# Two-instruction products of mLSTM weights and values over a pair of PSUM banks, and 512-column output banks in the projections of a hybrid encoder layer

## The chip, the cores and the metric

The kernel runs on one core of a Trainium2 chip. The metric is device time in microseconds (us) of one execution. Before the change the median of three runs is 2720.48 us (2719.08 to 2722.17).

## The reference, cut to what matters

One encoder layer is applied to two sequences, `x_prompt` (1024 tokens) and `x_sample` (2048 tokens), each with 16 learned meta tokens in front. A combined input projection (1024 to 6672 columns) feeds two branches, a neighbourhood attention and a bidirectional mLSTM; each is gated, projected, merged with the other by sigmoid gates and sent through one output projection with a normalisation and a residual.

```python
xn = _rmsnorm(h, g_pre)
proj = xn @ w_in + b_in.astype(xn.dtype)
...
ya = (ya.reshape(B, L, NA_WIDTH) * jax.nn.silu(na_z)) @ w_a
yb = (_mlstm_branch(ml_qk, ml_v, ml_g, ml_o, ml_conv_w, ml_head_g) * jax.nn.silu(ml_z)) @ w_b
ga, gb = jnp.split(jax.nn.sigmoid(mg), 2, axis=-1)
y = (ga * ya + gb * yb) @ w_out
return h + _rmsnorm(y, g_post)
```

In the mLSTM, 4 heads of 128 run over the tokens in chunks, forward and backward. The output of a chunk has a part from within the chunk, the weighted scores `S` times the values, and a part from the state carried in from the other chunks:

```python
S = jnp.einsum('bhnjd,bhnsd->bhnjs', q, k) * jnp.exp(logD - m_t[..., None])
e_inter = jnp.exp(inter - m_t)
num = jnp.einsum('bhnjs,bhnsv->bhnjv', S, v) + e_inter[..., None] * jnp.einsum('bhnvk,bhnjk->bhnjv', Cs, q)
```

## The kernel before

**Numbers in two parts.** TensorE (PE) multiplies in a reduced float32 (`F32R`). To keep float32 accuracy, each operand is split into a high part (a copy by ScalarE, ACT) and a low part (the difference, by VectorE, DVE), and a product is three matmuls: high by high, high by low, low by high. `mm3` (L170 to L174) issues these three; the first operand is the one that is loaded into the array, the second is streamed.

**Dense and sparse work.** `run` interleaves two Python generators. `sparse` walks through `STEPS`: mLSTM of the short sequence, its attention, mLSTM of the long sequence, its attention. `dense` walks through `PLAN`: input projections of groups of 512 tokens, then `final` for each block of 512 tokens (two of the short sequence, four of the long one). Each `yield` names a cost, and `run` lets dense work follow sparse work in the ratio of `rate`. PE executes in exactly this program order (`manual_schedule`); the order on the other engines and on the DMA queue of SyncE (SP) is chosen by the scheduler from a simulation, and where `behind` is called it keeps program order.

**PSUM.** There are 8 banks of 512 columns of float32. `psum` (L166) hands them out by tag: `pj` has 3 (projections), `tr` has 2 (transposes and others), `sc` has 1 (scores), and `sm` has 2 (small products: gates, states, the products of `back`, and the attention's scores and outputs).

**mLSTM outputs.** `ml_outputs` goes over blocks of 256 tokens (`CB` = 2 chunks of 128). In five steps per block it runs `scores(b)`, `back(b-1, 0)` and `weigh(b)`, `split` and `mask`, `back(b-1, 1)` with `values(b)` and `state(b)`, then `decay` and `finish`; between the steps dense matmuls run. `scores` (L1799, L1801) multiplies keys and queries in a 256-column and a 128-column matmul for each chunk. `weigh` makes the weighted scores in parts `sh` and `sl`. `values` makes `vh` and `vl`, 130 columns for each chunk: 128 of values, one of ones for the denominator, one of zeros. `back` makes the state's part in a `tr` bank, scales it into `num` with ACT (L1829), then takes an `sm` bank and issues three 130-column matmuls for each of two directions; DVE adds all 260 columns to `num` at L1834. `finish` divides by the denominators. `ml_states` makes the states' increments in the same way, one `sm` bank for each chunk, read by ACT (L1715) and DVE (L1717).

**Token-major projections.** `tm_unit` (matmuls at L644 to L646) computes 256 or 264 columns of the projection for tiles of 128 tokens. Each tile takes a `pj` bank and is evacuated by one DVE addition of the bias (L661 for the long sequence); two tiles share one buffer `stT` and one store.

**The end of the layer.** `final` has two stages for each block of 512 tokens. The first projects both branches (`mm3` with 512 columns, weight units `("m", f)`) and merges them into `mh` and `ml`. The second, the out stage, multiplies by `w_out`: `prods` (L2042 to L2044) issues 12 matmuls of 256 columns for one token tile and one weight unit, `("o", c, a)`, where `c` is the quarter of the 1024 columns and `a` the half of the contraction. Before, the loop goes over quarters `cq`, halves `a`, and four token tiles; a quarter holds two banks, each with two token tiles. `leave` squares with ACT (L2047, summing for the norm) and multiplies by the gain with DVE (L2048). In the last block the last two quarters are done tile by tile.

**Weights.** `wpump` keeps at most four weight units (`NBW` = 4, buffers `whi` and `wlo`) in flight. The first use of a unit loads it raw, splits it, and stores both parts (512 KB each); later uses load both parts (L264, on SP). `wtake` hands out the next unit, `wdone` frees one and pumps.

Of the kernel before, what the change touches and what calls it, by code (L numbers as in the profile page):

```python
# [126 lines left out]
class K:  # L127
# [38 lines left out]
    def psum(self, tag, shape):  # L166
        return self.pp.tile(shape, F32, name=tag, tag=tag, bufs=BANKS[tag])

# [8 lines left out]
    def setup(self, ctx):  # L177
        tc, nc, i = self.tc, self.nc, self.i
        self.cp = cp = ctx.enter_context(tc.tile_pool(name="cp", bufs=1))
        self.dp = dp = ctx.enter_context(tc.tile_pool(name="dp", bufs=1, space=DRAM))  # L180
        self.pp = ctx.enter_context(tc.tile_pool(name="pp", bufs=2, space=PSUM))
        self.ident = cp.tile([P, P], F32, name="ident")
# [436 lines left out]
    def tm_unit(self, col, halves, wd):  # L619
# [10 lines left out]
        for j, (x, s, c, n, cnt, tok) in enumerate(todo):  # L630
            st = wp.tile([P, 2, WU], F32, name="stT", bufs=4)
            for a in range(cnt):
                p = self.psum("pj", [P, 512])
                o = p[:n, :wd]
                xs = slice(c + a * P, c + a * P + n)
                for k in range(KT):
                    wh, wl = ws[k // 4][0][:, k % 4, :], ws[k // 4][1][:, k % 4, :]
                    if tok is None:
                        both = [(p[:48, :wd], self.xmm[:, k, :], wh), (o, self.xmm[:, k, :NM], wl)]
                        for y, (out, lhs, rhs) in enumerate(both if k < KT - 1 else both[::-1]):  # L640
                            nc.tensor.matmul(out, lhs, rhs, start=k == y == 0, stop=k == KT - 1 and y == 1, skip_group_check=True)
                    else:
                        xh, xl = x[0][:, k, xs], x[1][:, k, xs]
                        nc.tensor.matmul(o, xh, wh, start=k == 0, stop=False)  # L644
                        nc.tensor.matmul(o, xh, wl, start=False, stop=False)  # L645
                        nc.tensor.matmul(o, xl, wh, start=False, stop=k == KT - 1)  # L646
# [10 lines left out]
                elif s == 0:  # L657
                    r = tok // P + a
                    nc.vector.scalar_tensor_tensor(st[:n, a, :wd], p[:n, :wd], self.rc[:n, r:r + 1], bb[:n, :wd], op0=ALU.mult, op1=ALU.add)
                else:  # L660
                    nc.vector.tensor_tensor(st[:n, a, :wd], p[:n, :wd], bb[:n, :wd], op=ALU.add)  # L661
                if a == cnt - 1:
                    self.tm_store(col, wd, s, n, cnt, tok, st)
# [764 lines left out]
    def ml_gates(self, s, keep, mp, res):  # L1428
# [34 lines left out]
        def one(d):  # L1463
            l2 = lf[:, d].rearrange("p c h -> p (c h)")
            pb = self.psum("sm", [P, 512])
            nc.tensor.matmul(pb[:, :NR], self.tri[:, d, :], l2, start=True, stop=True)
# [14 lines left out]
            end = P - 1 if d == 0 else 0  # L1481
            pg = self.psum("sm", [P, 512])
# [4 lines left out]
            px = self.psum("sm", [P, 512])  # L1487
            nc.tensor.transpose(px[0:1, :NR], cm[:, end:end + 1], self.ident[:NR, :NR])
# [14 lines left out]
            yield  # L1503
            pm = self.psum("sm", [P, 512])
            nc.tensor.transpose(pm[:NR, 0:1], mpv, self.ident[0:1, 0:1])
# [11 lines left out]
            yield  # L1517
            pu = self.psum("sm", [P, 512])
            nc.tensor.transpose(pu[:, :NR], uR, self.ident[:NR, :NR])
# [6 lines left out]
            for name, x in (("e", cm), ("w", aR)):  # L1526
                pe = self.psum("sm", [P, 512])
                nc.tensor.transpose(pe[:, :NR], x, self.ident[:NR, :NR])
# [3 lines left out]
                yield  # L1532
            pf = self.psum("sm", [P, 512])
            nc.tensor.matmul(pf[:, :NR], self.ones[:NR, :], dg, start=True, stop=True)
# [62 lines left out]
    def ml(self, s):  # L1597
# [3 lines left out]
        with tc.tile_pool(name=f"mg{s}", bufs=1, side="right", reuse_waits="tile") as keep:  # L1601
            with tc.tile_pool(name=f"mt{s}", bufs=1, side="right", reuse_waits="tile") as mp:
# [6 lines left out]
                yield from self.ml_gates(s, keep, mp, g)  # L1609
            with tc.tile_pool(name=f"ml{s}", bufs=1, side="right", reuse_waits="tile") as mp:  # L1610
                self.vas = [mp.tile([P, CB, 130], F32, name=f"va{j}") for j in range(3)]
# [19 lines left out]
                while norms:  # L1631
# [3 lines left out]
                    yield A_A  # L1635
        self.done.add(("ml", s))

    def vload(self, mp, s, h, tok, np_, nch):
# [7 lines left out]
    def ml_states(self, mp, s, h, g, NB, sts):  # L1646
# [34 lines left out]
        for i in range(N):  # L1681
# [25 lines left out]
            if b:  # L1707
                sts[b - 1] = mp.tile([P, CB, 260], F32, name="st", bufs=NB)
            for j in range(CB - 1, -1, -1):
                cc = b * CB + j  # L1710
                pd = self.psum("sm", [P, 512])
                self.mm3(pd[:, :260], kth[:, j, :], ktl[:, j, :],
# [8 lines left out]
    def ml_outputs(self, mp, s, h, g, NB, sts, norms):  # L1721
# [96 lines left out]
        def back(b, j):  # L1818
            sh, sl = shs[b]
            (vh, vl), qx = vs[b], qks[b][:, 0]  # L1820
            cch, ccl = cs[b]
# [6 lines left out]
            for d in range(2):  # L1828
                nc.scalar.activation(num[:, j, d], pi[:, 130 * d:130 * d + 130], AF.Copy, scale=g[d]["e"][:, cc, h:h + 1])  # L1829
            pa = self.psum("sm", [P, 512])  # L1830
# [3 lines left out]
            nc.vector.tensor_tensor(nj, pa[:, :260], nj, op=ALU.add)  # L1834

# [129 lines left out]
    def final(self, s, b, nxt):  # L1965
# [55 lines left out]
        yt = [fp.tile([P, D], F32, name="yo", tag="xr", bufs=4) for _ in range(4)]  # L2021
        ssq = fp.tile([P, 4, 4], F32, name="ssq", bufs=2)
        sqj = fp.tile([P, 256], mybir.dt.bfloat16, name="sqj", tag="thT", bufs=1)
        hook = None
# [20 lines left out]

        def leave(o, tt, cq):
            nc.scalar.activation(sqj, o, AF.Square, accum_out=ssq[:, tt, cq:cq + 1])  # L2047
            nc.vector.tensor_tensor(yt[tt][:, cq * 256:(cq + 1) * 256], o, self.gpost[:, cq * 256:(cq + 1) * 256], op=ALU.mult)  # L2048

        for cq in range(4 if nxt else 2):  # L2050
            banks = [self.psum("pj", [P, 2, 256]) for _ in range(2)]
            for a in range(2):
                w = self.wtake(1)[0]
                for tt in range(4):
                    prods(banks[tt // 2][:, tt % 2], tt, w, a, tt % 2 == 0)
                    if tt == 3:
                        self.wdone()
                    if a and tt % 2:
                        for t in (tt - 1, tt):
                            leave(banks[t // 2][:, t % 2], t, cq)  # L2060
                        if nxt and hook is None:
# [5 lines left out]
                    if hook:  # L2067
                        next(hook, None)
                    yield 12 * C256
        if not nxt:  # L2070
            ws = [[self.wtake(1)[0] for _ in range(2)] for _ in range(2)]
            for tt, cq in [(0, 2), (1, 2), (0, 3), (1, 3), (2, 2), (2, 3), (3, 2), (3, 3)]:
                o = self.psum("pj", [P, 512])[:, :256]
                for a in range(2):
                    prods(o, tt, ws[cq - 2][a], a, True)
                    if a == 0:
                        yield 12 * C256
                leave(o, tt, cq)
                if cq == 3:
# [187 lines left out]
```

## Time and profile before

| | |
|---|---|
| median of three runs | 2720.48 us |
| the profiled execution's own time | 2718.74 us |
| its span, first to last instruction | 2717.0 us |
| granted TensorE clock, mean | 0.998 |
| DMA | 657.53 MB, mean 242 GB/s |
| out stages of `final`, first start to last end of L2042 to L2044 | 2056.1 to 2117.5, 2177.1 to 2240.8, 2303.0 to 2370.4, 2431.7 to 2493.0, 2553.0 to 2614.9, 2662.8 to 2708.7 us |
| additions of L1834, starts of the first and the last | 665.8 and 1977.8 us |

Busy time counts the union of the instructions of an engine. Matmuls overlap, so a busy PE says that it wasn't waiting, and the price of a matmul is the distance to the start of the next one. "PEld" is the weight load, which runs beside matmuls. In a group line the columns are busy us, the mean ns of one, and the idle time of the engine before them with what ended it.

### The profile page before, as it was taken

Reading aid. Unit: us, or ns where it says so; the run is one execution under the profiler, and the core shown is the slowest. Engines: PE = TensorE matmul, PEld = TensorE weight load, DVE = VectorE, ACT = ScalarE, POOL = GpSimd, SP = SyncE. Lnnn points to the kernel's source line nnn. Section 1 sums busy time; section 2 is a strip of 40 time slices with the busy share of each in tenths; the row PEclk is TensorE's granted clock in tenths of the full one; section 3 lists DMA queues with packets and bytes.
Section 4 is the critical chain, followed back from the end, with each engine's and each line's share of the span. In section 5 each row is a group of like instructions: output and inputs, shape, how many; then the busy total and the mean of one; then the engine's idle time right before and its main releaser. Section 6 shows DMA issues by size and latency. Waiting matters only on the chain.

```text
span 2717.0 us, 47583 instructions
## 1 busy us (share of the span) xinstructions
PE 2686.7 (99%) x16696; PEld 2394.5 (88%) x16696; DVE 1766.1 (65%) x4376; ACT 1520.2 (56%) x3375; POOL 126.0 (5%) x294
## 2 busy tenths in 40 slices
PE   9999999999999999999999999999999999999998
PEld 7999988879998889998878888888879898989988
DVE  5557765535777747775424857574658879687864
ACT  5233354435555656666535757564648686767641
POOL 0005000005000013000000000000000000000000
PEclk9999999999999999999999999999999999999999
DMA  9984454369865797757486666786599999898955
GB/s 369 340 283 143 138 187 158 102 239 343 265 222 174 264 325 227 229 175 234 144 294 191 222 202 209 262 278 201 163 299 332 313 298 295 245 317 244 324 208 220
DMA packets 351507, 657.53 MB, mean 242 GB/s; under 512 B 53444, under 2 KB 158868, under 8 KB 351268
## 3 DMA queue, kind: packets, MB, share of 16 engines
q1 hardware_dynamic: 344004, 645.46, 71.7%
q0 software_dynamic: 7264, 9.04, 1.2%
q8 instruction: 131, 2.15, 0.3%
q14 instruction: 108, 0.88, 0.1%
HBM read 438.64 MB, written 215.66 MB: 241 GB/s over the span
## 4 chain that ended last, share of the span: by engine, by line
PE 88%; DMA 7%; DVE 2%; ACT 2%; issue 1%; SPq 1%; POOL 0%; DVEq 0%; ACTq 0%; POOLq 0%
PE pj L172 14%; PE pj L173 14%; PE pj L174 14%; PE pj L644 5%; PE pj L645 5%; PE pj L646 5%; PE sm L1407 3%; PE pj L2042 2%; PE pj L2044 2%; PE pj L2043 2%; PE tr L1393 2%; PE sm L174 2%; PE sm L173 2%; PE sm L172 2%; DMA wraw<-wu 1%; DMA wlo<-wl 1%
## 5 line engine op out<-in xcount | busy, mean ns | idle before, releaser
L172 PE MATMUL pj<-xh,whi 128*128 128x512 f32 (+1 forms) x1480 | 580.2, 392 | 4.6 <-ACT st L569 3.6
L173 PE MATMUL pj<-xl,whi 128*128 128x512 f32 (+1 forms) x1480 | 565.8, 382 | 0.2 <-DVE xl L345 0.2
L174 PE MATMUL pj<-xh,wlo 128*128 128x512 f32 (+1 forms) x1480 | 565.1, 382 | 0.3 <-DVE wlo L272 0.3
L644 PE MATMUL pj<-whi,xh 128*128 128x256 f32 (+1 forms) x1152 | 330.9, 287 | 0.0
L174 PEld LDWEIGHTS pj<-xh,wlo 128*128 128x128 f32 x1480 | 278.2, 188 | 58.2 <-DVE wlo L272 0.6
L172 PEld LDWEIGHTS pj<-xh,whi 128*128 128x128 f32 x1480 | 278.5, 188 | 54.1 <-ACT st L569 4.4
L645 PE MATMUL pj<-wlo,xh 128*128 128x256 f32 (+1 forms) x1152 | 325.0, 282 | 0.6 <-DMA wlo<-wl 0.6
L646 PE MATMUL pj<-whi,xl 128*128 128x256 f32 (+1 forms) x1152 | 324.8, 282 | 0.0
L173 PEld LDWEIGHTS pj<-xl,whi 128*128 128x128 f32 x1480 | 278.8, 188 | 46.2 <-issue 0.7
L2042 PE MATMUL pj<-whi,mh 128*128 128x256 f32 x768 | 220.3, 287 | 0.0
L645 PEld LDWEIGHTS pj<-wlo,xh 128*128 128x128 f32 x1152 | 217.1, 188 | 0.9 <-DMA wlo<-wl 0.8
L644 PEld LDWEIGHTS pj<-whi,xh 128*128 128x128 f32 x1152 | 217.3, 189 | 0.4
L646 PEld LDWEIGHTS pj<-whi,xl 128*128 128x128 f32 x1152 | 217.0, 188 | 0.0
L2043 PE MATMUL pj<-wlo,mh 128*128 128x256 f32 x768 | 217.0, 283 | 0.0
L2044 PE MATMUL pj<-whi,mlo 128*128 128x256 f32 x768 | 216.9, 282 | 0.0
L1396 DVE TENSOR_TENSOR pts<-tr,pts 96x384 fp32r<-96x384 f32 (+2 forms) x192 | 118.5, 617 | 64.7 <-ACT pts L1395 63.8
L172 PE MATMUL pj<-yh,whi 128*128 128x512 f32 x384 | 154.2, 401 | 1.8 <-DVE tg L2009 1.1
L173 PE MATMUL pj<-yl,whi 128*128 128x512 f32 x384 | 151.0, 393 | 0.2 <-DVE yl L1420 0.2
L174 PE MATMUL pj<-yh,wlo 128*128 128x512 f32 x384 | 151.0, 393 | 0.0
L2043 PEld LDWEIGHTS pj<-wlo,mh 128*128 128x128 f32 x768 | 146.1, 190 | 1.0
L2042 PEld LDWEIGHTS pj<-whi,mh 128*128 128x128 f32 x768 | 146.0, 190 | 1.0
L2044 PEld LDWEIGHTS pj<-whi,mlo 128*128 128x128 f32 x768 | 145.9, 190 | 0.0
(459 smaller groups left out, 6171.7 us busy)
## 6 DMA issues: line engine op xcount, KB each, us to landing
whi<-wh SPq DMA_DIRECT2D x140, 512.0 KB
wlo<-wl SPq DMA_DIRECT2D x140, 512.0 KB
wraw<-wu SPq DMA_DIRECT2D x64, 512.0 KB
wh<-whi SPq DMA_DIRECT2D x64, 512.0 KB
wl<-wlo SPq DMA_DIRECT2D x64, 512.0 KB
gt<-st SPq DMA_DIRECT2D x96, 256.0 KB
tg<-gt SPq DMA_DIRECT2D x96, 256.0 KB
xt<-xt SPq DMA_DIRECT2D x32, 512.0 KB
```

The source lines that it names most:

```text
L172: mm(out, ah, bh, start=start, stop=False, **more)
L173: mm(out, ah, bl, start=False, stop=False, **more)
L174: mm(out, al, bh, start=False, stop=stop, **more)
L644: nc.tensor.matmul(o, xh, wh, start=k == 0, stop=False)
L645: nc.tensor.matmul(o, xh, wl, start=False, stop=False)
L646: nc.tensor.matmul(o, xl, wh, start=False, stop=k == KT - 1)
L1393: nc.tensor.transpose(pt[:ks, ch, :], pr_[:, ch * ks:(ch + 1) * ks], self.ident)
L1396: nc.vector.tensor_tensor(pts[:ks, :nb, 1, :], pt[:ks, :nb], pts[:ks, :nb, 0, :].bitcast(F32), op=ALU.subtract)
L1407: nc.tensor.matmul(av[:, cb % 2], vt[:ks, kc // 8 + ch].rearrange("p a b -> p (a b)"), pts[:ks, ch].rearrange("p a b -> p (a b)"), start=c ...
L2042: nc.tensor.matmul(o, mh[:, f, xs], q, start=fresh and f == 0, stop=False, skip_group_check=True)
L2043: nc.tensor.matmul(o, mh[:, f, xs], w[1][:, k, :], start=False, stop=False, skip_group_check=True)
L2044: nc.tensor.matmul(o, ml[:, f, xs], q, start=False, stop=f == KT - 1, skip_group_check=True)
```

## The change

Four things change.

1. **The product of `back`.** High and low parts of the values stand side by side in one tile, 260 columns. For each direction, one matmul takes the low weights by the high values (130 columns), and one takes the high weights by 258 columns, high values and 128 columns of low values. Each direction has its own bank, in a two-bank tile `pa` with a single buffer, and DVE adds columns 0 to 130 and then columns 130 to 258 of both banks to `num`.
2. **The pool of small banks.** `sm` becomes a pool of its own. It is closed while the mLSTM runs, and the two banks are then one two-bank tile, which `ml_states` uses too (one bank for each chunk of a block). The small products of `ml_gates` go to `tr`.
3. **`tm_unit`.** Where two tiles fit into a bank (256 columns, long sequence), both go into one `pj` bank and one DVE addition evacuates both.
4. **The out stage of `final`.** The loop goes over halves of the columns (512), pairs of token tiles, and four weight units; each token tile has its own bank of 512 columns, and `leave` works on 512 columns. In the last block the second half is done tile by tile as before, with `ssq` of three columns.

```diff
     def psum(self, tag, shape):
-        return self.pp.tile(shape, F32, name=tag, tag=tag, bufs=BANKS[tag])
+        return (self.pm if tag == "sm" else self.pp).tile(shape, F32, name=tag, tag=tag, bufs=BANKS[tag])
+
+    def small(self, on):
+
+        if on:
+            self.sms = ExitStack()
+            self.pm = self.sms.enter_context(self.tc.tile_pool(name=f"pm{len(self.done)}", bufs=2, space=PSUM))
+        else:
+            self.sms.close()
...
+            pair = s and tok is not None and 2 * wd <= 512
             for a in range(cnt):
-                p = self.psum("pj", [P, 512])
-                o = p[:n, :wd]
+                if not pair or not a:
+                    p = self.psum("pj", [P, 512])
+                o = p[:n, wd * a:wd * a + wd] if pair else p[:n, :wd]
...
+                elif a:
+                    two = bb[:, :wd].rearrange("p (t c) -> p t c", t=1).to_broadcast([P, 2, wd])
+                    nc.vector.tensor_tensor(st[:, :, :wd], p[:, :2 * wd].rearrange("p (t c) -> p t c", t=2), two, op=ALU.add)
...
+            self.small(False)
+            with tc.tile_pool(name=f"ml{s}", bufs=1, side="right", reuse_waits="tile") as mp, \
+                 tc.tile_pool(name=f"pl{s}", bufs=1, space=PSUM) as self.pl:
...
+            pds = self.pl.tile([P, CB, 512], F32, name="pa")
             for j in range(CB - 1, -1, -1):
                 cc = b * CB + j
-                pd = self.psum("sm", [P, 512])
+                pd = pds[:, j]
...
-                vh = mp.tile([P, CB, 130], F32R, name="vh", bufs=1)
-                vl = mp.tile([P, CB, 130], F32R, name="vl", bufs=1)
-                nc.scalar.activation(f2(vh), f2(va), AF.Copy)
-                nc.vector.tensor_tensor(f2(vl), f2(va), f2(vh).bitcast(F32), op=ALU.subtract)
-                vs[b] = vh, vl
+                v = vs[b] = mp.tile([P, CB, 2, 130], F32R, name="vh", bufs=1)
+                nc.scalar.activation(v[:, :, 0], va, AF.Copy)
+                nc.vector.tensor_tensor(v[:, :, 1], va, v[:, :, 0].bitcast(F32), op=ALU.subtract)
...
-            pa = self.psum("sm", [P, 512])
+            pa = self.pl.tile([P, 2, 512], F32, name="pa")
             for d in range(2):
-                self.mm3(pa[:, 130 * d:130 * d + 130], sh[:, j, d, :], sl[:, j, d, :], vh[:, j, :], vl[:, j, :])
-            nj = num[:, j].rearrange("p d c -> p (d c)")
-            nc.vector.tensor_tensor(nj, pa[:, :260], nj, op=ALU.add)
+                nc.tensor.matmul(pa[:, d, 0:130], sl[:, j, d, :], v[:, j, 0], start=True, stop=False, skip_group_check=True)
+                nc.tensor.matmul(pa[:, d, 0:258], sh[:, j, d, :], v[:, j].rearrange("p a c -> p (a c)")[:, 0:258], start=False, stop=True, skip_group_check=True)
+            nj = num[:, j]
+            nc.vector.tensor_tensor(nj, pa[:, :, 0:130], nj, op=ALU.add)
+            nc.vector.tensor_tensor(nj[:, :, 0:P], pa[:, :, 130:258], nj[:, :, 0:P], op=ALU.add)
...
-        for cq in range(4 if nxt else 2):
-            banks = [self.psum("pj", [P, 2, 256]) for _ in range(2)]
-            for a in range(2):
-                w = self.wtake(1)[0]
-                for tt in range(4):
-                    prods(banks[tt // 2][:, tt % 2], tt, w, a, tt % 2 == 0)
-                    if tt == 3:
-                        self.wdone()
-                    if a and tt % 2:
-                        for t in (tt - 1, tt):
-                            leave(banks[t // 2][:, t % 2], t, cq)
...
+        for cp in range(2 if nxt else 1):
+            ws = []
+            for pair in range(2):
+                banks = [self.psum("pj", [P, 512]) for _ in range(2)]
+                for u in range(4):
+                    if not pair:
+                        ws.append(self.wtake(1)[0])
+                    for t in range(2):
+                        tt, o = 2 * pair + t, 256 * (u // 2)
+                        prods(banks[t][:, o:o + 256], tt, ws[u], u % 2, u == 0)
+                        if pair and t:
+                            self.wdone()
+                        if u == 3:
+                            leave(banks[t], tt, 512 * cp, 512, cp)
```

More of the change, by code (lines that the diff above doesn't have):

```diff
@@ L181, in setup @@
         self.pp = ctx.enter_context(tc.tile_pool(name="pp", bufs=2, space=PSUM))
+        for tag in ("pj", "tr", "sc"):
+            self.psum(tag, [P, 512])
+        self.small(True)
+        ctx.callback(lambda: self.small(False))
         self.ident = cp.tile([P, P], F32, name="ident")
@@ L643, in tm_unit @@
                         xh, xl = x[0][:, k, xs], x[1][:, k, xs]
-                        nc.tensor.matmul(o, xh, wh, start=k == 0, stop=False)
-                        nc.tensor.matmul(o, xh, wl, start=False, stop=False)
-                        nc.tensor.matmul(o, xl, wh, start=False, stop=k == KT - 1)
+                        nc.tensor.matmul(o, xh, wh, start=k == 0 and not (pair and a), stop=False, skip_group_check=True)
+                        nc.tensor.matmul(o, xh, wl, start=False, stop=False, skip_group_check=True)
+                        nc.tensor.matmul(o, xl, wh, start=False, stop=k == KT - 1, skip_group_check=True)
                     if k == 3:
@@ L659, in tm_unit @@
                     nc.vector.scalar_tensor_tensor(st[:n, a, :wd], p[:n, :wd], self.rc[:n, r:r + 1], bb[:n, :wd], op0=ALU.mult, op1=ALU.add)
-                else:
+                elif not pair:
                     nc.vector.tensor_tensor(st[:n, a, :wd], p[:n, :wd], bb[:n, :wd], op=ALU.add)
+                elif a:
+                    two = bb[:, :wd].rearrange("p (t c) -> p t c", t=1).to_broadcast([P, 2, wd])
+                    nc.vector.tensor_tensor(st[:, :, :wd], p[:, :2 * wd].rearrange("p (t c) -> p t c", t=2), two, op=ALU.add)
                 if a == cnt - 1:
@@ L1472, in one @@
             yield
-            pa = self.psum("sm", [P, 512])
+            pa = self.psum("tr", [P, 512])
             nc.tensor.transpose(pa[:NR, :P], aTf, self.ident)
@@ L1517, in one @@
             yield
-            pu = self.psum("sm", [P, 512])
+            pu = self.psum("tr", [P, 512])
             nc.tensor.transpose(pu[:, :NR], uR, self.ident[:NR, :NR])
@@ L1636, in ml @@
         self.done.add(("ml", s))
+        self.small(True)
     def vload(self, mp, s, h, tok, np_, nch):
@@ L1697, in ml_states @@
             if not c0:
-                pd = self.psum("sm", [P, 512])
+                pd = self.pl.tile([P, 2, 512], F32, name="pa")[:, 0]
                 self.mm3(pd[:, :130], kth[:NM, 0, :], ktl[:NM, 0, :], vwh[:NM, 0, 0, :], vwl[:NM, 0, 0, :])
@@ L1819, in back @@
             sh, sl = shs[b]
-            (vh, vl), qx = vs[b], qks[b][:, 0]
+            v, qx = vs[b], qks[b][:, 0]
             cch, ccl = cs[b]
@@ L2021, in final @@
         yt = [fp.tile([P, D], F32, name="yo", tag="xr", bufs=4) for _ in range(4)]
-        ssq = fp.tile([P, 4, 4], F32, name="ssq", bufs=2)
-        sqj = fp.tile([P, 256], mybir.dt.bfloat16, name="sqj", tag="thT", bufs=1)
+        ssq = fp.tile([P, 4, 3], F32, name="ssq", bufs=2)[:, :, :2 if nxt else 3]
+        sqj = fp.tile([P, 512], mybir.dt.bfloat16, name="sqj", tag="thT", bufs=1)
         hook = None
@@ L2044, in prods, with leave @@
                 nc.tensor.matmul(o, ml[:, f, xs], q, start=False, stop=f == KT - 1, skip_group_check=True)
[L2046 to L2061 removed]
+        def leave(o, tt, c0, n, q):
+            nc.scalar.activation(sqj[:, :n], o, AF.Square, accum_out=ssq[:, tt, q:q + 1])
+            nc.vector.tensor_tensor(yt[tt][:, c0:c0 + n], o, self.gpost[:, c0:c0 + n], op=ALU.mult)
+        for cp in range(2 if nxt else 1):
[12 more added lines that the diff above has]
+                            leave(banks[t], tt, 512 * cp, 512, cp)
+                        if nxt and hook is None and u == 2:
                             if nxt[0] != "f":
@@ L2066, in final @@
                                 hook = self.ystart(*nxt[1:])
-                    if hook:
-                        next(hook, None)
-                    yield 12 * C256
+                        if hook:
+                            next(hook, None)
+                        yield 12 * C256
         if not nxt:
@@ L2077, in final @@
                         yield 12 * C256
-                leave(o, tt, cq)
+                leave(o, tt, 256 * cq, 256, cq - 1)
                 if cq == 3:
```

15 lines of the change are left out of this document (6 added, 9 removed).

## The prediction

> **What bounds the kernel now.** I read the head of the profile first, then the groups by line with shapes kept apart, the order of time around one product, and the waits.
>
> ```profile
> span 2717.0 us, 47583 instructions
> PE 2686.7 (99%) x16696; PEld 2394.5 (88%) x16696; DVE 1766.1 (65%) x4376; ACT 1520.2 (56%) x3375; POOL 126.0 (5%) x294
> PE 88%; DMA 7%; DVE 2%; ACT 2%; issue 1%; SPq 1%; POOL 0%; DVEq 0%; ACTq 0%; POOLq 0%
> ```
>
> The tensor engine (PE) is idle for 2717.0 - 2686.7 = 30.3 us in all. So work taken off VectorE (DVE) or ScalarE (ACT) can give back at most a part of these 30 us, and matmul time taken off PE shortens the span directly, as long as nothing new makes PE wait. Three edits bear on time: the packed product in `back`, the shared banks of `tm_unit`, and the 512-column banks of `final`.
>
> **The packed product.** Before, `back` computes weights times values for each direction in three 130-column matmuls with three weight loads:
>
> ```profile
> L174 PE MATMUL sm<-vh,sl 128*128 128x130 f32 x192 | 52.9, 276 | 0.0
> L173 PE MATMUL sm<-vl,sh 128*128 128x130 f32 x192 | 52.7, 274 | 0.0
> L172 PE MATMUL sm<-vh,sh 128*128 128x130 f32 x192 | 48.0, 250 | 0.0
> ```
>
> 192 of each are 96 products of two directions (12 blocks of 256 tokens over both sequences, 4 heads, 2 chunks). The mean of one, 276 ns, is no price: matmuls overlap. The price is the distance between starts, which the order of time gives (start, duration):
>
> ```profile
> 663.96 0.23 PE L172 MATMUL sm<-vh,sh 128*128 128x130 f32 x1
> 664.03 0.27 PE L173 MATMUL sm<-vl,sh 128*128 128x130 f32 x1
> 664.14 0.28 PE L174 MATMUL sm<-vh,sl 128*128 128x130 f32 x1
> 664.25 0.28 PE L172 MATMUL sm<-vh,sh 128*128 128x130 f32 x1
> ...
> 664.58 0.33 PE L644 MATMUL pj<-whi,xh 128*128 128x256 f32 x1
> 664.75 0.28 PE L645 MATMUL pj<-wlo,xh 128*128 128x256 f32 x1
> 664.87 0.28 PE L646 MATMUL pj<-whi,xl 128*128 128x256 f32 x1
> ```
>
> Here 130 columns cost 0.11 us (664.03 to 664.14) and 256 columns 0.12 us (664.75 to 664.87). The narrow one is not paid by its columns but by the weight load that must come before the next matmul. The six take 664.58 - 663.96 = 0.62 us, and the dense matmul behind them starts its successor after 0.17 instead of 0.12 us, so the product costs 0.67 us. After the change each direction is one 130-column and one 258-column matmul. The trace has the same alternation, in the scores:
>
> ```profile
> 661.72 0.28 PE L1799 MATMUL sc<-qkx 128*128 128x256 f32 x1
> 661.84 0.22 PE L1801 MATMUL sc<-qkx 128*128 128x128 f32 x1
> 661.90 0.33 PE L1799 MATMUL sc<-qkx 128*128 128x256 f32 x1
> 662.07 0.22 PE L1801 MATMUL sc<-qkx 128*128 128x128 f32 x1
> 662.13 0.34 PE L644 MATMUL pj<-whi,xh 128*128 128x256 f32 x1
> 662.30 0.28 PE L645 MATMUL pj<-wlo,xh 128*128 128x256 f32 x1
> ```
>
> Four matmuls: 662.13 - 661.72 = 0.41, plus 0.05 behind them, is 0.46 us. I take 0.46 for the new product. The saving is 0.21 us, times 96 = 20 us. Its bounds: nothing, if the columns alone counted (390 before and 388 after), and 192 removed matmuls x 0.11 = 21 us, if the widening is free.
>
> [...]
>
> **What the packed product adds.** A second DVE addition folds columns 130 to 258 in, and both banks are now one tile with a single buffer, where two single-bank buffers took turns. So the product for chunk j=1 of a block must wait until both additions of chunk j=0 are done. Behind that matmul the whole PE queue waits, dense work included. The prices:
>
> ```profile
> L1834 DVE TENSOR_TENSOR num<-sm,num 128x260 f32<-128x260 f32 x96 | 40.5, 423 | 62.5 <-ACT num L1829 59.6 <-ACT vwh L1671 2.6
> 905.00:945.00 40.00, 40.00 (x213) 33.99 (x212) 37.66 (x103) 28.05 (x65) 2.92 (x12) 1.00 0.64 200
> 1763.08 0.22 PE L172 MATMUL sm<-vh,sh 128*128 128x130 f32 x1
> 1766.89 0.23 PE L172 MATMUL sm<-vh,sh 128*128 128x130 f32 x1
> 1764.17 0.43 DVE L1834 TENSOR_TENSOR num<-sm,num 128x260 f32<-128x260 f32 x1 [1.12 <-ACT num L1829]
> 915.08 0.23 PE L172 MATMUL sm<-vh,sh 128*128 128x130 f32 x1
> 918.90 0.22 PE L172 MATMUL sm<-vh,sh 128*128 128x130 f32 x1
> 921.95 0.75 DVE L1834 TENSOR_TENSOR num<-sm,num 128x260 f32<-128x260 f32 x2
> ```
>
> (The second line is a stretch: start and end, its length, then busy us of PE, weight loads, DVE, ACT and GpSimd, the granted clock, the DMA share and GB/s.) The usual pair of backs looks like the one at 1763: the addition ends at 1764.60, the next product starts at 1766.89, and a second addition of 0.42 still leaves 1.9 us. The exception is 905 to 945, the last head of the short sequence, where DVE is busy 37.66 of 40 us. The first product is at 915.08, the second at 918.90, and the addition comes only at 921.95, merged with the next one. With one buffer PE would stand until about 922.8, an estimate of 3.5 to 4 us. That stall lets DVE catch up, so it isn't paid at each of the four pairs there. The other check is DVE's work: 8 more additions x 0.42 = 3.4 us on 37.66 make 41.1 in a stretch that should shrink to 38. Both readings give 3 to 4 us; I add 1 to 2 for smaller ones elsewhere and take 5, between 0 (the scheduler, which orders DVE with the new wait in view, moves the additions forward) and 12 (each late pair pays in full).
>
> The states' products use the same pair of banks; their readers come at once, and the next block's products follow two steps of dense work later, so I cost them at nothing (cover: that dense work; without it each of the 48 blocks would wait for one more read of a bank, some 0.4 us by the row of L1834). The gates' small products move to tag "tr", which has two buffers as "sm" had: nothing.
>
> **The shared banks of `tm_unit`.** PE issues the same matmuls. For the long sequence's 256-wide columns two DVE additions become one:
>
> ```profile
> L661 DVE TENSOR_TENSOR stT<-pj,bb 128x256 f32<-128x256 f32 x96 | 40.3, 420 | 27.9 <-PE pj L646 26.2 <-DMA nv<-stT 0.6
> L1940 DVE TENSOR_TENSOR yl<-yl,yh 128x512 fp32r<-128x512 f32 x43 | 28.2, 682 | 1.5 <-ACT yh L1956 1.4
> L2048 DVE TENSOR_TENSOR yo<-pj,gain 128x256 f32<-128x256 f32 x96 | 40.3, 419 | 38.7 <-ACT sqj L2047 38.1
> ```
>
> 48 x (2 x 0.42 - 0.68) = 7.7 us of DVE work go, beside PE. A bank is asked for half as often. Nothing on the path.
>
> **The banks of `final`.** Again the same matmuls. The evacuations of 256 columns become 44 of 512 and 8 of 256, 7 us of DVE work less, nothing on the path by itself. What counts is when things come free. In the out stage each weight unit now serves two token tiles, then all four are used again by the other two. Before, a unit was read by four tiles in one go, and a freed buffer had the time of three more units to be refilled. Now four units are freed one after another in the second half, and each is needed three half-units later.
>
> ```profile
> 2056.00:2118.00 62.00, 61.02 (x508) 60.73 (x507) 49.81 (x114) 51.51 (x125) 0.00 (x0) 1.00 1.00 338
> 2553.00:2615.00 62.00, 61.66 (x508) 61.05 (x507) 41.32 (x103) 43.47 (x113) 0.00 (x0) 1.00 0.74 239
> 2663.00:2709.00 46.00, 45.72 (x384) 45.52 (x382) 17.23 (x64) 7.93 (x32) 0.00 (x0) 1.00 0.48 179
> kx<-masks POOLq DMA_DIRECT2D x2, 256.0 KB, 6.2
> ACT sqj L2047 <- PE pj L2044: 43.9, 28, 7.1
> DVE yo L2048 <- ACT sqj L2047: 38.1, 39, 7.2
> ```
>
> The out stage takes 62 us for 8 units, 7.75 us each, so the lead falls from 3 x 7.75 = 23 to 3 x 3.9 = 11.6 us; in the last one (46 us, no attention beside it) from 17 to 8.6. A unit is two parts of 512 KB, 1.05 MB. The transfers whose landing this stretch shows took 6.2 us for 256 KB. In the second half of a pair four units, 4.2 MB, are asked for in 15.5 us, 271 GB/s, on top of other traffic: 239 - 135 = 104 GB/s in the fifth out stage and some 200 in the first, where DMA is already fully busy at 338. So the backlog grows by up to 4 us in a half, and landing at 6 to 10 us meets a lead of 11.6: mostly in time. I take 3 us for 11 such halves, between 0 and 25. The bank's hand-over shrinks too: with three banks, the first bank of a pair is wanted two half-units (3.9 us) after its last matmul. ACT's square and DVE's product read it one after the other, as the last two lines show; that is about 1.5 us of work, with waits of up to 7.2. I take 2 us, between 0 and 8.
>
> **The sum**, on the profiled execution (2718.7 us, span 2717.0): 2718.7 - 20 + 5 + 3 + 2 = 2708.7; the 1.7 us around the span stay. The median of the runs shown, 2720.5, is 1.8 above that execution, so the forecast is 2710.
>
> **The rivals.**
>
> *No new wait* (2700). The product is packed and all hand-overs are covered: 2720.5 - 20. For it: the usual slack of 1.9 us and PE's small idle time. Against it: the stretch at 905.
>
> *DVE's queue eats most of it* (2721). If the single pair of banks costs its upper 12 us and the finals 8, the gain is gone. For it: DVE at 94% at 905 and additions that already come late there; against it: elsewhere in the outputs DVE has room.
>
> *Weights come late in the finals* (2735, slower). Place: the second half of each pair in `final`; mechanism: weight units queue behind other transfers and land after their 11.6 us. It decides from landings of over 11.6 us; with 5 us lost at the banks of `back`, a mean of 1.4 us in each of the 11 halves cancels the gain, and 1.9 us makes the kernel slower by over 0.2%. If they land at 14.3 us, the 10 us above with the 4 us of backlog on top, each half waits 2.7 us, 30 in all, and the time is 2720.5 - 20 + 5 + 30 = 2735. For it: the first out stage's DMA share of 1.00; against it: 0.74 and 0.48 in the later ones.
>
> [...]
>
> **How the numbers follow.** Forecast (2704 to 2715) 0.42, no new wait (2699 to 2704) 0.23, DVE's queue 0.18, late weights 0.12, columns 0.05. 0.2% is 5.4 us, about what a measurement of this kernel can tell from no change: faster is below 2715.0, the first two cases, 0.65; same holds the DVE case, 0.18; slower the last two, 0.17. The range 2699 to 2724 leaves out the late weights, part of the columns' case and a little at the lower end.
>
> **What would show it.** PE should issue 192 matmuls fewer (16504), and `back` should show 130 and 258 columns with 0.46 us from its first start to the dense work's regular step. A wait of a 130-column matmul on DVE at `back`, most of it near 920, is the step of 5 us. Waits of the out stage's matmuls on a DMA of weights, or on DVE at the product with the gain, are the steps of 3 and 2 us. I am wrong if PE's busy time falls by much less than 20 us, or if PE's idle time grows by more than 20 us beyond its 30.

## The result, and the profile after

The changed kernel takes 2782.65 us (median of 4 runs, 2779.64 to 2794.05), the kernel before beside it 2721.32. The ratio is 1.0242, with a 95% interval of 1.0224 to 1.026: slower by 61 us, where 10 us less had been forecast, and 59 us above the range.

The head of the profile after:

```profile
span 2778.6 us, 47126 instructions
PE 2693.1 (97%) x16504; PEld 2386.9 (86%) x16504; DVE 1794.4 (65%) x4380; ACT 1515.9 (55%) x3287; POOL 125.3 (5%) x294
PE 83%; DVE 6%; DMA 6%; ACT 3%; issue 1%; SPq 1%; POOL 0%; DVEq 0%; ACTq 0%; POOLq 0%
```

The 192 matmuls are gone (16504 of 16696). Idle time of PE is now 2778.6 - 2693.1 = 85.5 us; it was 30.3. DVE's share of the chain that ended last rose from 2% to 6%. The list of who waited for whom on PE (total us, times, longest) names the place:

```profile
PE pa L180 <- DVE st L1738: 43.1, 48, 2.5
PE pa L1851 <- DVE num L1855: 8.7, 6, 5.4
PE pj L2064 <- DMA wlo<-wl: 2.3, 1, 2.3
```

The first line is neither the product of `back` (that is L1851) nor the out stage (L2064). L180 with the tile `pa` is the first matmul of a state's product in `ml_states`, and it waits 48 times, once for each block of 256 tokens in each head. The order of time in one of these blocks shows how (weight loads left out):

```profile
725.12 0.28 PE L180 MATMUL pa<-vwh,kt 128*128 128x260 f32 x1
725.24 0.28 PE L181 MATMUL pa<-vwl,kt 128*128 128x260 f32 x1
725.36 0.28 PE L182 MATMUL pa<-vwh,kt 128*128 128x260 f32 x1
725.68 0.28 ACT L1736 ACTIVATE st<-pa 128x130 f32<-128x130 f32 x1 [3.73 <-PE pa L182]
725.99 0.35 DVE L1738 SCALAR_TENSOR_TENSOR st<-st,g_fb,pa 128x130 f32<-128x130 f32 x1 [1.70 <-ACT st L1736]
...
726.39 0.39 PE L180 MATMUL pa<-vwh,kt 128*128 128x260 f32 x1 [0.76 <-DVE st L1738]
```

The three matmuls of chunk 1 go into one bank; ACT reads it, then DVE; and only then, at 726.39, does the product of chunk 0 start, although it goes into the other bank. In the kernel before, the next start came 0.12 us after the third matmul:

```profile
706.87 0.28 PE L174 MATMUL sm<-vwh,kt 128*128 128x260 f32 x1
706.99 0.28 PE L172 MATMUL sm<-vwh,kt 128*128 128x260 f32 x1
```

Here it comes after 1.03. Over the 48 blocks the starts lie 51.4 us further apart than 0.12 us each (from 0.67 to 2.64 more, median 0.92). The first matmul behind the wait then takes 0.23 us to the next start in the mean, where it took 0.12. From the first start of a block's six matmuls to the start of the next work, the 48 blocks take 93.7 us in all, and took 37.6: 56.1 us more. The two banks were two tiles before; now they are one.

The packed product does what was forecast:

```profile
682.86 0.30 PE L1851 MATMUL pa<-vh,sl 128*128 128x130 f32 x1 [0.58 <-DVE ss L447]
683.00 0.34 PE L1852 MATMUL pa<-vh,sh 128*128 128x258 f32 x1
683.17 0.23 PE L1851 MATMUL pa<-vh,sl 128*128 128x130 f32 x1
683.24 0.33 PE L1852 MATMUL pa<-vh,sh 128*128 128x258 f32 x1
683.40 0.29 PE L658 MATMUL pj<-whi,xh 128*128 128x264 f32 x1
```

Counted as in the prediction, from the first start to the dense work's regular step, it takes 0.466 us in the median of the 96 (0.671 before). Its mean is 0.490 (0.673 before), 17.5 us less in all. The wait in the first of these lines is the other one that was expected, for DVE's additions (the second of them, L1855, ran from 682.30 to 682.71; the profile names the DVE instruction behind it): the second chunk's product starts late, by 16.1 us over the 48 blocks. The longest of these waits, 5.6 us, ends at 943.94. What stands before it on the other engines is ACT's scaling of the state's part into `num`, here for both chunks, and the two additions of chunk 0:

```profile
940.50 1.13 ACT L1848 ACTIVATE num<-tr,g_eT 128x130 f32<-128x130 f32 x4
941.89 0.42 DVE L1854 TENSOR_TENSOR num<-pa,num 128x260 f32<-128x260 f32 x1
943.38 0.41 DVE L1855 TENSOR_TENSOR num<-pa,num 128x256 f32<-128x256 f32 x1
```

A third loss was not in the forecast. Stretches of the profile after (start and end, length, then busy us of PE, weight loads, DVE, ACT, GpSimd, the granted clock, DMA share, GB/s):

```profile
716.00:720.00 4.00, 2.01 (x16) 1.80 (x15) 1.90 (x5) 2.97 (x10) 0.00 (x0) 0.98 0.84 259
720.00:723.00 3.00, 3.00 (x15) 3.00 (x15) 1.86 (x6) 1.39 (x5) 0.00 (x0) 0.50 0.99 314
942.00:949.00 7.00, 5.06 (x15) 4.21 (x16) 5.90 (x17) 3.37 (x8) 0.81 (x2) 0.53 0.55 169
```

PE was busy 2.01 of 4 us, with a wait of 2.0 us that ends at 718.51, and for the 3 us behind it the granted clock is 0.50. Beside the wait of 5.4 us that ends at 943.94 stands 0.53 over 942 to 949. Four such stretches come before the first `final`, at 211, 720, 942 and 1775; that at 942 lasts 6.8 us, the others 3.4, together 17.1. The kernel before has none there (its clock is 1.00 up to 2339). At half rate they cost at most 17.1 / 2 = 8.5 us, an estimate. The one at 211 need not come from the change: ahead of it stand two waits of 1.05 and 1.10 us for DVE (up to 208.93 and 210.38), and the kernel before has the same two, of 0.89 and 1.09 us (up to 209.24 and 210.69), with a granted clock of 1.00 behind them.

The sum: 56.1 for the states' products + 16.1 at the second chunk - 17.5 for the product + 2.1 for all `final` blocks (715.5 us from the first start to the end of the span, 713.4 before) = 56.8, of 61.6 us between the two spans. The 4.8 us left lie within the 8.5 that the clock can cost at most.

### The profile page after: what moved, and what is told of

Same layout as the page of the kernel before. It is cut to its first block, busy times and chain, and to the rows that moved or that the text cites. A ratio compares the mean times of both kernels' runs of the same rounds, so it can differ in the third digit from the quotient of the medians.

```text
span 2778.6 us, 47126 instructions
## 1 busy us (share of the span) xinstructions
PE 2693.1 (97%) x16504; PEld 2386.9 (86%) x16504; DVE 1794.4 (65%) x4380; ACT 1515.9 (55%) x3287; POOL 125.3 (5%) x294
## 4 chain that ended last, share of the span: by engine, by line
PE 83%; DVE 6%; DMA 6%; ACT 3%; issue 1%; SPq 1%; POOL 0%; DVEq 0%; ACTq 0%; POOLq 0%
PE pj L180 13%; PE pj L181 13%; PE pj L182 13%; PE pj L658 5%; PE pj L659 5%; PE pj L660 5%; PE pj L2064 3%; PE pj L2065 3%; PE pj L2063 3%; PE sm L1424 3%; PE tr L1410 2%; PE pa L1852 1%; PE pa L180 1%; PE sm L182 1%; PE sm L180 1%
## 5 line engine op out<-in xcount | busy, mean ns | idle before, releaser
L180 PE MATMUL pj<-xh,whi 128*128 128x512 f32 (+1 forms) x1480 | 578.0, 391 | 3.2 <-ACT st L581 2.9
L180 PEld LDWEIGHTS pj<-xh,whi 128*128 128x128 f32 x1480 | 279.4, 189 | 52.8 <-ACT st L581 3.6
L2064 PE MATMUL pj<-wlo,mh 128*128 128x256 f32 x768 | 217.9, 284 | 3.8 <-DMA wlo<-wl 2.3
L180 PE MATMUL pj<-yh,whi 128*128 128x512 f32 x384 | 154.1, 401 | 0.7 <-ACT yh L1436 0.7
L2064 PEld LDWEIGHTS pj<-wlo,mh 128*128 128x128 f32 x768 | 146.5, 191 | 5.2 <-DMA wlo<-wl 2.6
```

The source lines that it names most:

```text
L180: mm(out, ah, bh, start=start, stop=False, **more)
L2064: nc.tensor.matmul(o, mh[:, f, xs], w[1][:, k, :], start=False, stop=False, skip_group_check=True)
```

## The experiments

The theory after these readings: **the state tile**. With both chunks' banks in one tile, the second chunk's matmul has to wait for the readers of the first, which the program issues between the two. The rivals: **the single buffer** (the pair of banks comes free too late from block to block, whatever the order), and **the product or the out stage**, which the prediction had feared.

**The order inside a block (e1_order).** The changed kernel, with both chunks' matmuls ahead of the readers.

```diff
             for j in range(CB - 1, -1, -1):
+                self.mm3(pds[:, j, :260], kth[:, j, :], ktl[:, j, :],
+                         vwh[:, j].rearrange("p d c -> p (d c)"), vwl[:, j].rearrange("p d c -> p (d c)"))
+            for j in range(CB - 1, -1, -1):
                 cc = b * CB + j
                 pd = pds[:, j]
-                self.mm3(pd[:, :260], kth[:, j, :], ktl[:, j, :],
-                         vwh[:, j].rearrange("p d c -> p (d c)"), vwl[:, j].rearrange("p d c -> p (d c)"))
```

> The changed kernel, except that ml_states issues the matmuls of both chunks of a block before the readers of either; tiles, banks and buffers stay. Theory (one tile for two chunks): the second chunk's matmul waits for the readers of the first chunk only because they are issued between the two and share the tile; the 51 us between the chunks go, with some 5 us of half-rate clock, and the time is 2720 to 2730. Rival (one buffer): the wait is for the pair of banks to come free from the block before, whatever the order inside a block; the time stays within 10 us of 2782 and the wait moves to the first chunk's matmul.

It took 2727.49 us, 55 less than the changed kernel; the ratio to the kernel before is 1.003 (1.0018 to 1.0042). The group of the first matmul of a state's product (idle time before it at the end) had 43.6 us of idle time in the changed kernel (first line) and has 1.8 here (second line):

```profile
L180 PE MATMUL pa<-vwh,kt 128*128 128x260 f32 x96 | 32.4, 338 | 43.6 <-DVE st L1738 43.1 <-ACT kt L1710 0.5
L180 PE MATMUL pa<-vwh,kt 128*128 128x260 f32 x96 | 27.5, 286 | 1.8 <-DVE st L1739 1.1 <-ACT kt L1710 0.5 <-ACT vh L1793 0.3
```

Tile, banks and buffer are the same, so the single buffer is not the cause.

**The states' tile alone (e2_states).** The kernel before, with `pds = self.pl.tile([P, CB, 512], F32, name="pa")` and `pd = pds[:, j]` in `ml_states`. The small banks get a pool of their own for it, and the gates' products go to `tr`; nothing else of the change is in it.

> The kernel before with the states' two-bank tile alone; the products of back keep their three matmuls and two single banks, out stage and tm_unit as before. Theory (one tile for two chunks): 2765 to 2780, with about 50 us of waits of the second chunk's matmul on DVE. Rival (the loss lies in the products of back or in the out stage): 2718 to 2726.

2775.85 us, ratio 1.0209 (1.0186 to 1.0232). The waits of PE:

```profile
PE pa L180 <- DVE st L1734: 41.8, 48, 2.4
```

This one edit costs 57.6 us, of the 61 that the whole change costs.

**Two tiles in the same places (e11_two_tiles).** As the last one, in the order of the change, but with each bank a tile of its own.

```diff
-            pds = self.pl.tile([P, CB, 512], F32, name="pa")
+            pds = [self.pl.tile([P, 512], F32, name=f"pa{j}") for j in range(CB)]
...
-                pd = pds[:, j]
+                pd = pds[j]
```

> The kernel before with the states' products in the same two banks, single buffer, and in the order of the change (matmul, readers, matmul, readers), but with each bank a tile of its own. Theory (the wait is for the tile, not for the bank): the 42 us of waits go and the time is 2716 to 2724. Rival (the order inside a block or the single buffer makes the wait): 2765 or more.

2719.49 us, ratio 1.0006 (0.9997 to 1.0015), no difference from before.

```profile
L180 PE MATMUL pa<-vwh,kt 128*128 128x260 f32 x96 | 27.4, 285 | 0.3 <-ACT kt L1706 0.3
```

The pools are those of e2_states; only the tiles differ. So the order alone costs nothing here, and the single buffer next to nothing in e1_order (1.1 us of waits for DVE). The wait belongs to the tile: with one tile for both banks (e2_states) the framework made a matmul into one half wait for the readers of the other, 41.8 us in all; with two tiles there is no such wait.

**The packed product alone (e5_product).** The kernel before with the product of `back` and the two-bank tile of the change, and the states' matmuls in the order of e1_order.

> The kernel before with the packed product of back and the two-bank tile, states' matmuls of both chunks ahead of their readers; out stage and tm_unit as before. Theory: 17.5 us are saved by two loads and matmuls fewer per product, some 16 us are lost where the second chunk's product waits for DVE's additions, and the time is 2716 to 2726. Rival (the packed product alone is slower): over 2730. Rival (it gains in full): 2700 to 2708.

2722.34 us, ratio 1.0012 (1.0001 to 1.0022). The product takes 0.466 us in the median, as in the changed kernel. The second chunk's products start 17.0 us late in all, 5.6 of it once, at 926:

```profile
PE pa L1847 <- DVE num L1851: 10.1, 8, 5.5
PE pa L1847 <- DVE mv L1924: 2.1, 2, 1.2
PE pa L1847 <- DVE mv L1922: 1.8, 2, 1.2
```

The last two lines are waits for the additions as well; the profile names a DVE instruction that ended behind them.

The saving is given back where it was feared, by three times the 5 us that were taken.

**More time for DVE (e6_balanced).** As e5_product, with chunk 0's product half a step earlier.

```diff
                 scores(b)
-            yield A_A
+            yield A_A / 2
             if p >= 0:
                 back(p, 0)
+            yield A_A / 2
             if b < NB:
                 weigh(b)
```

> The packed product alone (kernel before, packed product, two-bank tile, states' matmuls ahead of their readers), with chunk 0's product half a step earlier, ahead of weigh, so that DVE has 4.8 instead of 3.9 us between the products of one block, and 4.8 instead of 5.7 to the next. Theory (the saved 17.5 us are given back because the one pair of banks comes free too late for the second chunk): the waits on DVE at the second chunk fall from 17 us to below 9, and the time is 2705 to 2716. Rival (DVE is simply behind around 926 and elsewhere, and the place does not matter): waits of 14 us or more, time as without the shift, 2717 to 2726.

The late starts fell from 17.0 to 8.7 us, as expected, but the time is 2720.43 us (ratio 1.0008, 0.9996 to 1.0019), above what the theory gave and not distinguishable from e5_product. A wait of the states on the pair of banks, and waits of the attention, hold 13.8 us in this profile (2.1, 6.9 and 1.7, together 10.7, in that of e5_product):

```profile
PE sm L1419 <- ACT prb L1388: 5.0, 2, 3.7
PE pa L180 <- DVE st L1734: 4.8, 4, 2.7
PE pa L1847 <- DVE num L1851: 4.8, 5, 2.4
PE sm L1419 <- DVE yg L1426: 4.0, 4, 2.2
```

What became of the 8 us is only partly told by these lines, and stays open. So this run shows that the place of the product sets its waits, and not that they were the whole loss.

**Without the second addition (e7_no_low).** As e5_product; the product of high weights and low values is computed but left out of the sum.

> The packed product alone, without the second addition (the product of high weights and low values is left out of the sum). Theory as in the prediction (a second addition of 0.42 us on a late bank costs little beside the single buffer): the waits at the second chunk fall from 17 us to about 10, the time is 2710 to 2718. Rival (the second addition makes the wait): they fall to below 4 us and the time is 2702 to 2708.

2709.43 us, ratio 0.9964 (0.9948 to 0.9979); late starts of 6.7 us.

```profile
PE pa L1847 <- DVE num L1850: 5.2, 5, 3.7
```

Neither theory has it right: 10 of the 17 us go with the second addition (its own time and the 40 us of work that DVE has less in all), and 7 stay with the single buffer.

**One direction packed (e8_one_dir).** The kernel before; one direction keeps three matmuls, the other takes two. 130 + 130 + 128 columns fit one bank, so the two single banks take turns as before.

```diff
-                self.mm3(pa[:, 130 * d:130 * d + 130], sh[:, j, d, :], sl[:, j, d, :], vh[:, j, :], vl[:, j, :])
+                x, o = v[:, j].rearrange("p a c -> p (a c)"), pa[:, 130 * d:130 * d + 130]
+                nc.tensor.matmul(o, sl[:, j, d, :], x[:, 0:130], start=d == 0, stop=False, skip_group_check=True)
+                if d == 0:
+                    nc.tensor.matmul(o, sh[:, j, d, :], x[:, 0:130], start=False, stop=False, skip_group_check=True)
+                    nc.tensor.matmul(o, sh[:, j, d, :], x[:, 130:260], start=False, stop=True, skip_group_check=True)
+                else:
+                    nc.tensor.matmul(pa[:, 130:388], sh[:, j, d, :], x[:, 0:258], start=False, stop=True, skip_group_check=True)
```

> The kernel before with the packed product for one direction only (130 columns, 130 columns for the other direction's high part, 128 for the packed low part), which fits one bank, so that the two single banks take turns as before; states, tm_unit and out stage as before. Theory (without the single pair of banks the packed product pays): one of two matmuls and loads saved, 8 to 10 us less on PE, no wait of the product on DVE, 2706 to 2714. Rival (the second DVE addition or something else of the packing costs time by itself): 2717 or more.

2713.81 us, ratio 0.9979 (0.9965 to 0.9992): this version beats both kernels, the one before by 0.2%. The product's mean is 0.577 us, 9.2 us less than before in all, and no product starts late. Both additions are there (the last numbers are idle time of the engine before them):

```profile
L1838 DVE TENSOR_TENSOR num<-sm,num 128x260 f32<-128x260 f32 x96 | 40.5, 424 | 48.8 <-ACT num L1827 48.4
L1839 DVE TENSOR_TENSOR num<-sm,num 128x128 f32<-128x128 f32 x96 | 27.2, 286 | 1.3
L1831 PE MATMUL sm<-vh,sl 128*128 128x130 f32 x192 | 47.9, 250 | 0.0
```

A second addition, here of 128 columns and 0.286 us, makes no product late where the next one has a bank of its own; with the pair it sits on the path. Of the 9.2 us, 4.7 show in the medians; where the rest went is not known.

**The out stage alone (e3_final).** The kernel before with the new loop of `final`.

> The kernel before with the new out stage of final alone. Theory (the states cost the time, the out stage is covered): within 5 us of before, 2716 to 2726. Rival (weights come late in the finals): 2735 or more, with PE waiting for DMAs of weights at the out stage.

2727.38 us, ratio 1.0027 (1.0014 to 1.0039): slower by more than the theory allowed and by less than the rival wanted. Waits of the out stage that the kernel before doesn't have, and the first out stage, 66 us long where it had been 61.4:

```profile
PE pj L2043 <- DMA wlo<-wl: 3.3, 1, 3.3
PE pj L2043 <- DVE wlo L272: 1.4, 1, 1.4
PE pj L2042 <- DMA whi<-wh: 1.0, 1, 1.0
2057.40:2123.50 66.10, 63.07 (x506) 62.03 (x505) 49.15 (x106) 50.40 (x110) 0.00 (x0) 0.97 0.90 309
```

Of these waits only that on DVE, which splits the fresh weights (1.4 us, at 2103), lies in the first out stage; a stretch at half rate begins there (granted clock 0.97 in the mean of the stage). The waits on DMA lie in the second (1.0) and the third (3.3).

**The new out stage in all blocks but the first (e9_final_later).** The old loop where `self.fresh` holds, the new one elsewhere.

> The kernel before with the new out stage in all blocks but the first, whose weights come raw and are split by ACT and DVE on the way. Theory (the out stage's loss of 9 us is weights that come late, most of it where they are fresh and DMA is full): the first out stage is back at 61 to 62 us from 66, and the time is 2718 to 2724. Rival (the loss is spread over all blocks): 2726 or more.

2722.69 us, ratio 1.0018 (1.0008 to 1.0028). The first out stage, which has the old loop again, is back:

```profile
2060.50:2122.00 61.50, 60.35 (x499) 59.87 (x498) 48.94 (x114) 50.59 (x124) 0.00 (x0) 1.00 1.00 339
```

The second one went from 63.4 to 66.3 us, and PE waits for weights for 2.4 us there and 1.8 us in the third. The intervals of the two runs overlap, so the medians don't settle the share of the first block. The profiles of all kernels say more: with the old loop the first out stage took 60.2 to 61.6 us in ten profiles, with the new one 65.4 to 66.0 in three. The second took 63.7 to 68.2 us in nine profiles with the old loop and 62.4 to 66.3 in four with the new one, so its length tells nothing. The loss that the out stage's lengths show is therefore that of the first block, 4 to 6 us; the 5 us by which this run's median still lies above the kernel before are not explained. That late weights make waits in the out stage is shown, at some 4 to 6 us of waits, and not the 30 of the rival.

**The shared banks of `tm_unit`, alone (e4_tm) and beside one packed direction (e10_one_dir_tm).**

> The kernel before with the shared banks of tm_unit alone. Theory: no path, 2716 to 2724, that is within 0.2% of before. Rival (a bank held for two tiles, or the shifted evacuation, makes PE wait): 2728 or more, with waits of L644-like matmuls on DVE.

> The kernel before with the packed product for one direction (two single banks in turn) and the shared banks of tm_unit, which take 8 us of work off DVE. Theory (DVE's work is off the path where nothing waits for it): as the one direction alone, 2708 to 2716. Rival (less work on DVE shortens the remaining waits): below 2707.

Alone 2720.69 us (1.0005, 0.9995 to 1.0015); beside the one direction 2713.86 us (0.9983, 0.9973 to 0.9993), the same as without it. DVE's two additions of 420 ns became one of 686 (48 times), and nothing waited for them.

## Why the prediction was wrong, point by point

1. **What bounds the kernel: right,** but not the sign that was to show it. Both signs of being wrong came: PE's idle time grew by 55.2 us, and its busy time rose by 6.4 instead of falling by 20. The first is mostly the states' wait (43.1 us). The second does not speak against the product, because busy time grows with waits: a matmul counts for 0.28 us where its step is 0.12 (at 725.24), so its tail counts at every wait, and at half rate it counts for longer (0.63 us for the one at 944.94, where its group, L180 with 512 columns, has a mean of 0.40). In e2_states, with the 16696 matmuls of the kernel before, busy time rose by 21.0 us, to 2707.7.
2. **The product: right.** 0.46 us was read off the scores' four matmuls, 0.466 was measured; 17.5 us of the 20 came. That columns alone count, the case with a chance of 0.05, is refuted by the same number: by the columns, 390 before and 388 after, nothing would have been saved. No run shows a price that puts part of this case into the range.
3. **The states: here the prediction failed.** It said that "their readers come at once, and the next block's products follow two steps of dense work later", and costed them at nothing. It looked from block to block and not inside a block, where a matmul, its two readers and the next matmul stand in a row. That makes 56.1 us at the states' products, 1.17 us in each of 48 blocks; the edit alone costs 57.6 us (e2_states), and the loss goes with the order (e1_order) or with two tiles (e11_two_tiles). The price named for the case that the cover failed, 0.4 us for one read, was too small as well: two reads stand in the wait, one behind the other. No rival named this place, so the range missed it.
4. **The second chunk of `back`: right in kind and place, too small.** 5 us were taken, between 0 and 12; it was 16.1, with 5.6 us of it in one wait from 938 to 944, at the last head of the short sequence. The stretch where DVE was busy 37.66 of 40 us was the right one to look at, but DVE is only a part of that wait. The product of chunk 0 had started at 934.45, and ACT scaled the state's part into `num`, which the first addition needs, from 940.50 on; 2.2 of the 5.6 us pass before that. Other work of DVE then stands ahead of the two additions and between them. The larger error is in the small waits: 1 to 2 us were added for those elsewhere, and they make 10.5, none over 1.6. So the step that fell is that a second addition leaves 1.9 us of slack in the usual pair; 10 of 17 us go with that addition (e7_no_low).
5. **`tm_unit`: right,** no difference (e4_tm).
6. **The out stage: right in kind, for the weights.** 5 us were taken; alone it costs 9 (e3_final). Inside the change the `final` blocks took 715.5 us, which is not outside the 710.8 to 717.8 of the profiles with the old loop; only the first out stage is. The 2 us for the hand-over of banks are not seen: no matmul of the out stage waits for the product with the gain.
7. **The clock was missing.** Waits of 2 us and more were priced at their length; behind some of them PE ran at half rate for 3.4 us or more (a granted clock of 0.50 from 719.83 to 723.24).

Had the states cost nothing, the forecast would still have had the wrong sign: e1_order, which is the change without that wait, is slower by 0.3%, where 0.4% faster was forecast. By the medians, points 4 and 6 together took back more than the product saved.

## What to carry to other kernels

Before merging buffers into one tile, go through the program between two writes into it: whatever reads any part of it there stands between them, in another bank too (57.6 us here in e2_states, no difference with a tile for each bank in e11_two_tiles). Issue all writes ahead of the reads, or keep a tile for each bank. And when a matmul is saved at the price of a buffer, compare the saving with the wait at the busiest place of the engine that frees the buffer: here half of the saving, with the buffers left alone, beat the whole of it.

## What the runs showed of the hardware that had not been expected

The granted clock fell to 0.50 for 3.4 us from 719.83 on, behind a wait of PE of 2.0 us that ends at 718.51, and for 6.8 us from 941.70 on, in the last part of a wait of 5.4 us that ends at 943.94 and behind it. The four matmuls of one product took 944.94 - 943.94 = 1.0 us there, where 0.54 is the step in the lines at 682.86:

```profile
943.94 0.45 PE L1851 MATMUL pa<-vh,sl 128*128 128x130 f32 x1 [5.44 <-DVE num L1855]
944.19 0.52 PE L1852 MATMUL pa<-vh,sh 128*128 128x258 f32 x1
...
944.94 0.63 PE L180 MATMUL pj<-xh,whi 128*128 128x512 f32 x1
945.36 0.63 PE L181 MATMUL pj<-xl,whi 128*128 128x512 f32 x1
```

A 512-column matmul starts 0.42 us after the one before it, where the whole trace has a median of 0.23.

Why one wait has a fall behind it and another has none, the traces do not show. In the profile after, the wait of 2.08 us that ends at 1774.20 is followed by a fall at 1774.55, and the wait of 2.08 us that ends at 1754.34 by none. PE was busy for 1.93 us in the 4 us from 1770.55, ahead of that fall, and for 1.53 us in the 4 us from 1624.73, at whose end a wait of 2.47 us ends with a granted clock of 1.00 behind it (1626 to 1632).
